# Gates moved between the two halves of a head's q, k, v projection, in a gated attention layer on one NeuronCore

## The chip, the core and the metric

The kernel runs on one core of one Trainium2 chip. The time is the device time of one execution in microseconds (us); three runs are shown for the kernel before, and their median is the number to predict against. One further execution was recorded by the hardware profiler, and all rows below come from that one. Engines are called PE (TensorE matmul), DVE (VectorE), ACT (ScalarE), POOL (GpSimd) and SP (SyncE, which here only issues DMAs).

## The reference, cut to what matters

With DEPTH = 1 only the first layer runs: 1024 tokens, 1024 features, 16 heads with a value width of 128 and two query/key pairs of width 64 each.

```python
def diff_attention_layer(x, norm_g, w_in, q_norm_g, k_norm_g, ..., head_norm_g, w_out, layer_idx):
    h = rms_norm(x, norm_g)
    q, k, v, z = jnp.split(h @ w_in, 4, axis=-1)
    q = rms_norm(q.reshape(b, s, DA_HEADS, 2, DA_HEAD), q_norm_g) * (DA_HEAD ** -0.5)
    k = rms_norm(k.reshape(b, s, DA_HEADS, 2, DA_HEAD), k_norm_g)
    ...
        scores = einsum('bqhmd,bkhmd->bhmqk', qb, kb)          # per block of 128 queries, causal
        probs = softmax(scores + alibi_bias)
        weights = probs[:, :, 0] - lam * probs[:, :, 1]
        outs.append(einsum('bhqk,bkhe->bqhe', weights, vb))
    ...
    o = rms_norm(o, head_norm_g) * (1.0 - lam_0)
    o = o.reshape(b, s, BRANCH) * jax.nn.silu(z)
    return x + o @ w_out
```

## The kernel before, in words

**Products.** Each f32 operand is split into two f16 parts, hi and lo, and a product is three matmuls (hi·hi, hi·lo, lo·hi) that add up in PSUM. The normalised input stands transposed in SBUF as `h0` and `h1`, for the first and the last 512 tokens; index `c` is 0 or 1 for these halves.

**Prologue.** Eight tiles of x are normalised (`htok`, L259), transposed on PE (`tp`, L275) and split by ACT (L277) and DVE (L278) into `h`. The first head's projection starts before all eight are there: the scheduler puts its matmuls between the transposes.

**Heads.** They run in the order 1, 3, .., 15, 0, 2, .., 14. While head i is projected, head i−1 is attended: `merge` (L656) draws pieces of both by the costs that they yield and the rates in `RATE`; then the tile scheduler fixes the order of instructions on each engine. `project` (L354) does, for each half `c`: four token tiles, 24 matmuls each of 128x384 into a PSUM tile `pg` (L370 to L372); ACT copies q, k out (L422) and v (L423); DVE makes the low part of v, `vl` (L424). Then `norm(c, rw)`: ACT squares (L381), DVE sums (L383), POOL multiplies by the gain (L385), a small chain for 1/sqrt (L90 to L103), DVE multiplies (L388), ACT and DVE split (L391, L392), SP transposes (L393) and copies. After both halves come the gates: `gate(st, wt, 3, c)` (L443), 24 matmuls of 128x512 into `pz` (L447 to L449) and a chain of six steps that gives z·sigmoid(z) in `sz`: ACT exp (L452), DVE min (L453), ACT ln (L454), DVE (L455), ACT exp (L456), DVE (L457). `pz` is read by the last step, so its PSUM slot is free only then. `pg` and `pz` share one ring of three PSUM slots (`PSG` = 3, tag "pg").

The heads 10, 12, 14 (`LATE`) have no gates in `project`; `late_gates` (L510) computes them at the end, while head 14 is attended, and beside them splits the first half of `w_out` (`wo_half`, `split_wo`; DVE subtraction L467 into `wol`).

**Preparation of w_in.** The raw weights of the next head come by SP DMAs (L136) into the single buffer `raww`. `split_w` (L141) is a generator that `prepare` advances one step at a time: four squares on ACT (L160), a small chain with one PE matmul into spare columns of a `pg` tile (L169), then hi on ACT (L199), and lo on DVE (L205, blocks q and k) or on POOL (L202 and L203, blocks v and z). Before, it is advanced after each token tile and at every second step of the gates; the first head, which also has its own z block to prepare, advances it at each half tile.

**Attention.** `attend` (L540) goes through eight blocks of 128 queries: scores on PE (L570) into `pss` (four PSUM slots), DVE takes them out with the bias and a running minimum (L559), ACT exp (L576), DVE combines the two softmaxes (L581, L582, L584), ACT and DVE split (L66, L587), SP transposes. Values on PE (L601 to L603), then the head norm (L607 to L631, POOL L614) and `finalize` (L529), in which POOL multiplies with the gate (L537) and SP writes to DRAM.

**End.** The second half of `w_out` and the products with the gathered heads (`pf`, L498 to L500).

## Time and profile before

| | us |
|---|---|
| runs before | 1181.22, 1174.27, 1176.29 |
| median | 1176.29 |
| profiled execution, own time | 1173.53 |
| its span (first to last instruction) | 1171.8 |
| PE busy in the span | 1109.9 (95%) |
| DVE busy | 883.0 (75%) |
| ACT busy | 774.2 (66%) |
| POOL busy | 272.2 (23%) |

The profiled execution takes 1.7 us beyond its span and lies 2.8 us below the median. The mean clock that TensorE was granted over the span is 0.983 of full speed. A row of the timeline reads: start, duration, engine, line, operation, output<-inputs, and in brackets the idle time of that engine just before, with what ended it. Rows of waits read: engine, what it was about to write and its line, `<-` what it waited for, total us, times, longest.

### The profile page before, as it was taken

What the parts mean: (1) busy time and instruction counts of PE and PEld (TensorE: products, weight loads), DVE (VectorE), ACT (ScalarE), POOL (GpSimd) and SP (SyncE); (2) the same over time, 40 slices, a digit from 0 to 9 for tenths busy, and PEclk for the clock granted to TensorE, in tenths of its full rate; (3) what the DMA queues carried; (4) which work ended last, traced back from release to release, by engine and by line L of the source; (5) the groups of instructions that cost most, each with busy time, mean ns of one, the idle gap of its engine ahead of it and who ended that gap; (6) DMA issues with size and microseconds to landing.
All of it is one profiled execution on the core that took longest, in us unless ns stands there. A gap on an engine that the chain in (4) does not pass through costs nothing.

```text
span 1171.8 us, 18439 instructions
## 1 busy us (share of the span) xinstructions
PE 1109.9 (95%) x6154; PEld 668.5 (57%) x6154; DVE 883.0 (75%) x2180; ACT 774.2 (66%) x1713; POOL 272.2 (23%) x208
## 2 busy tenths in 40 slices
PE   4999999999999999999999999999899997999998
PEld 3555554545555555555545455555455534788887
DVE  6867869787978797879787878788888898563121
ACT  4757778787878797869686978787778776230000
POOL 2220314141314131314131313312121302031000
PEclk7999999999999999999999999999999988999999
DMA  7453736464646464646463645464564457685342
GB/s 222 109 119 52 164 67 140 89 140 85 139 90 137 88 143 89 146 80 133 93 144 76 140 93 126 93 129 100 105 137 87 109 125 182 143 292 179 112 130 70
DMA packets 327887, 143.50 MB, mean 122 GB/s; under 512 B 225136, under 2 KB 307312, under 8 KB 327792
## 3 DMA queue, kind: packets, MB, share of 16 engines
q1 hardware_dynamic: 323040, 133.93, 50.9%
q10 hardware_dynamic: 4752, 8.39, 2.7%
q8 instruction: 48, 0.79, 0.3%
q14 instruction: 47, 0.39, 0.1%
HBM read 63.11 MB, written 16.25 MB: 68 GB/s over the span
## 4 chain that ended last, share of the span: by engine, by line
PE 51%; DVE 20%; ACT 10%; issue 8%; DMA 6%; POOL 2%; SPq 2%; DVEq 0%; ACTq 0%; POOLq 0%
PE pg L370 8%; PE pg L371 8%; PE pg L372 8%; DVE p L559 6%; PE pf L498 5%; PE pf L499 5%; PE pf L500 5%; PE pss L570 3%; DMA raww<-in_l_w_in_dram 3%; DVE p L584 2%; ACT p L576 2%; ACT wsp L160 2%; ACT wsp L199 2%; DMA wt<-p 2%; PE po L601 2%
## 5 line engine op out<-in xcount | busy, mean ns | idle before, releaser
L370 PE MATMUL pg<-wsp,h 128*128 128x384 f16 x1024 | 336.3, 328 | 21.0 <-DVE sz L457 11.9
L372 PE MATMUL pg<-wsp,h 128*128 128x384 f16 x1024 | 336.4, 329 | 1.1 <-DVE h L278 1.1
L371 PE MATMUL pg<-wsp,h 128*128 128x384 f16 x1024 | 336.3, 328 | 1.2 <-POOL wsp L203 1.2
L576 ACT ACTIVATE p<-p,mn 128x128 f32<-128x128 f32 (+7 forms) x256 | 196.4, 768 | 61.0 <-DVE mn L559 59.8
L559 DVE CUSTOM_DVE_ANT_0 p<-pss,toep,nsl 128x512 f32<-128x512 f32 (+3 forms) x256 | 161.2, 642 | 36.8 <-DMA wt<-p 24.6
L570 PE MATMUL pss<-qk 128*128 128x512 f16 (+3 forms) x768 | 164.6, 327 | 11.6 <-DVE mn L559 11.5
L371 PEld LDWEIGHTS <-h 128*128 128x128 f16 x1024 | 100.7, 98 | 86.7 <-issue 26.5
L372 PEld LDWEIGHTS <-h 128*128 128x128 f16 x1024 | 100.6, 98 | 68.2 <-issue 3.7
L66 ACT ACTIVATE p<-p,rc 128x128 f16<-128x128 f32 (+7 forms) x128 | 98.6, 771 | 61.8 <-DVE p L584 60.7
L370 PEld LDWEIGHTS <-h 128*128 128x128 f16 x1024 | 100.7, 98 | 66.6 <-issue 4.1
L584 DVE SCALAR_TENSOR_TENSOR p<-p,rc,p 128x128 f32<-128x128 f32 (+7 forms) x128 | 116.9, 914 | 1.5
L587 DVE SCALAR_TENSOR_TENSOR p<-p,rc,p 128x128 f16<-128x128 f32 (+7 forms) x128 | 104.7, 820 | 14.8 <-ACT p L66 14.6
L570 PEld LDWEIGHTS <-qk 128*128 128x128 f16 x768 | 71.0, 98 | 72.2 <-issue 18.6
L447 PE MATMUL pz<-h,wsp 128*128 128x512 f16 x256 | 98.3, 384 | 1.3 <-DVE sz L457 1.3
L448 PE MATMUL pz<-h,wsp 128*128 128x512 f16 x256 | 98.3, 384 | 0.0
L614 POOL TENSOR_TENSOR sql<-sqo,sqh 128x512 fp32r<-128x512 f32 x30 | 41.7, 1390 | 243.3 <-ACT sqh L612 243.3
L449 PE MATMUL pz<-h,wsp 128*128 128x512 f16 x256 | 98.1, 383 | 0.0
L537 POOL TENSOR_TENSOR sz<-sqo,sz 128x512 f32<-128x512 f32 x26 | 37.7, 1448 | 184.4 <-DVE sqo L631 150.0
L202 POOL TENSOR_SCALAR raww<-raww,scw 128x1024 f32<-128x1024 f32 (+1 forms) x31 | 42.3, 1371 | 159.1 <-ACT wsp L199 127.9
L559 DVE CUSTOM_DVE_ANT_0 p<-pss,toep,mn 128x128 f32<-128x128 f32 (+3 forms) x128 | 75.6, 601 | 0.0
L160 ACT ACTIVATE wsp<-raww 128x1024 f16<-128x1024 f32 x61 | 63.6, 1044 | 14.7 <-DMA raww<-in_l_w_in_dram 9.4
L503 DVE TENSOR_TENSOR xr<-pf,xr 128x512 f32<-128x512 f32 (+1 forms) x33 | 22.1, 671 | 63.4 <-PE pf L500 62.5
(160 smaller groups left out, 2082.9 us busy)
## 6 DMA issues: line engine op xcount, KB each, us to landing
raww<-in_l_w_in_dram SPq DMA_DIRECT2D x96, 256.0 KB, 3.8
rawo<-in_l_w_out_dram SPq DMA_DIRECT2D x32, 256.0 KB, 4.5
qk<-qk SPq DMA_DIRECT2D x64, 128.0 KB, 2.4
raww<-in_l_w_in_dram SPq DMA_DIRECT2D x40, 192.0 KB, 3.7
g_dram<-sz SPq DMA_DIRECT2D x30, 256.0 KB, 2.3
rawg<-g_dram ACTq DMA_DIRECT2D x24, 256.0 KB, 3.5
xt<-in_x_dram SPq DMA_DIRECT2D x8, 512.0 KB, 5.3
xr<-in_x_dram SPq DMA_DIRECT2D x16, 256.0 KB, 3.5
```

The source lines that it names most:

```text
L66: A.activation(out, in_, AF.Copy, scale=scale)
L370: T.matmul(pg, a_h, w_h, start=k == 0, stop=False)
L371: T.matmul(pg, a_h, w_l, start=False, stop=False)
L372: T.matmul(pg, a_l, w_h, start=False, stop=k == KT - 1)
L447: T.matmul(pz, wt["hi"][:, k, n], hh[c][:, k], start=k == 0, stop=False)
L448: T.matmul(pz, wt["hi"][:, k, n], hl[c][:, k], start=False, stop=False)
L449: T.matmul(pz, wt["lo"][:, k, n], hh[c][:, k], start=False, stop=k == KT - 1)
L559: V.tensor_tensor_reduce(out=pm[m][:, o:o + w], in0=pss[:, :w], in1=toep[:, u:u + w], scale=nslope, scalar=3e38 if prev[m] is None else pr ...
L570: T.matmul(pss[m][:, :w].rearrange("p (t q) -> p t q", q=P), qk[:, c, 0, i % 4, m], qk[:, b, v, :w // P, m], start=v == 1, stop=v == 2)
L576: A.activation(pm[m][:, :n], pm[m][:, :n], AF.Exp, scale=-1.0, bias=prev[m], accum_out=sx[:, 1 - m:2 - m])
L584: V.scalar_tensor_tensor(out=p0, in0=p1, scalar=rc[:, 0:1], in1=p0, op0=ALU.mult, op1=ALU.add)
L587: V.scalar_tensor_tensor(out=pl[:, n:], in0=p0, scalar=rc[:, 1:2], in1=pl[:, :n], op0=ALU.mult, op1=ALU.subtract)
```

## The change

`project` is written in another order. `qkv(c)` is the former loop body. Heads outside `LATE` now run `qkv(0)`, both gates, `qkv(1)`; before, `qkv(0)`, `qkv(1)`, both gates. `prepare(None)` at half a tile is now called for every head, but only with c = 0: of the next head's preparation 8 calls stand in `qkv(0)`, 8 in the gates and 4 in `qkv(1)`. The ring of `sz` has four buffers instead of three. The temporary `sqo` of the head norm no longer has a tile of its own; it takes the first 512 columns of the ring "sqk" (2 buffers), which `norm` and the out-projection use. Lines from 441 on have a number lower by one in the changed kernel.

```diff
-            for c in range(2):
+            def qkv(c):
                 rw = tmp.tile([P, 2, 4, P], F32, name="rw", tag="rw", bufs=2)
                 for t in range(4):
...
                             prepare(lambda: pb[:, 384:])
-                        elif hd == heads[0]:
+                        elif c == 0:
                             prepare(None)
                         yield 2.1
                 norm(c, rw)
-            if hd in LATE:
-                while prep:
-                    prepare(None)
-                return
-            for c in range(2):
-                for k in gate(st, wt, 3, c):
-                    if k % 2:
-                        prepare(None)
-                    yield 0.69
+            yield from qkv(0)
+            if hd not in LATE:
+                for c in range(2):
+                    for k in gate(st, wt, 3, c):
+                        if k % 2:
+                            prepare(None)
+                        yield 0.69
+            yield from qkv(1)
             while prep:
                 prepare(None)
...
-            e = vp.tile([P, 512], F32, name="sz", tag="sz", bufs=3)
+            e = vp.tile([P, 512], F32, name="sz", tag="sz", bufs=4)
...
-                sq = tmp.tile([P, 512], F32, name="sqo", tag="sqo")
+                sq = tmp.tile([P, 1024], F32, name="sqo", tag="sqk", bufs=2)[:, :512]
```

What the scheduler makes of it, at three places. The numbers behind names tell buffers apart.

PE in the prologue, before: `tp_514` and `tp_521` are the transposes of the last x tile, `pg_766` and `pg_796` are tiles of the first head's half c = 1. Between `tp_507` and `tp_514` stand 26 matmuls here.

```order
L372 MATMUL pg_766<-wsp_206,h1_84 128x384
L169 MATMUL pg_722<-br_735,ones_63 128x4
L370 LDWEIGHTS h1_84
L370 MATMUL pg_796<-wsp_206,h1_84 128x384
L371 LDWEIGHTS h1_84
L371 MATMUL pg_796<-wsp_206,h1_84 128x384
L275 MATMUL tp_514<-ident_65,htok_498 128x128 x4
L275 MATMUL tp_521<-ident_65,htok_498 128x128 x4
```

The same place after; `pz_721` and `pz_755` are the gates of the first head.

```order
L448 MATMUL pz_721<-h0_83,wsp_206 128x512
L275 MATMUL tp_500<-ident_65,htok_405 128x128 x4
L275 MATMUL tp_507<-ident_65,htok_405 128x128 x4
L275 MATMUL tp_514<-ident_65,htok_498 128x128 x4
L275 MATMUL tp_521<-ident_65,htok_498 128x128 x4
L446 LDWEIGHTS wsp_206
L446 MATMUL pz_755<-h1_84,wsp_206 128x512
L370 LDWEIGHTS h1_84
L370 MATMUL pg_788<-wsp_206,h1_84 128x384
```

Now 24 gate matmuls stand ahead of the four transposes in a row (22 of them behind the transposes of the tile before), the second gate's first matmul right behind them, and the first head's c = 1 tiles after that.

DVE in a head of the middle, before: the end of gate 0's chain (`sz_5507`), up to the step that frees its PSUM slot.

```order
L388 TENSOR_TENSOR rw_5137<-rw_5137,r_k_5419 128x1024
L455 SCALAR_TENSOR_TENSOR sz_5507<-pz_5427,inv_4307,sz_5507 128x512
L581 RECIPROCAL rc_5535<-sums3_461 128x2
L582 TENSOR_TENSOR rc_5535<-rc_5535,sums3_461 128x2
L559 ISA p0_5558,mn_5567<-pss_5561,toep_407,nsl_432 128x128
L559 ISA mn_5567 128x1
L559 ISA p1_5559,mn_5569<-pss_5562,toep_407,nsl_432 128x128
L559 ISA mn_5569 128x1
L584 SCALAR_TENSOR_TENSOR p0_5481<-p1_5482,rc_5535,p0_5481 128x1024
L631 SCALAR_TENSOR_TENSOR sqo_5389<-os_5387,gh_416,sqo_5389 128x512
L392 TENSOR_TENSOR sqk_5407<-rw_5137,sqk_5407 128x16x64
L457 SCALAR_TENSOR_TENSOR sz_5507<-pz_5427,inv_4307,sz_5507 128x512
```

The same place after (`sz_5903`):

```order
L388 TENSOR_TENSOR rw_5585<-rw_5585,r_k_5812 128x1024
L454 SCALAR_TENSOR_TENSOR sz_5903<-pz_5820,inv_4935,sz_5903 128x512
L583 SCALAR_TENSOR_TENSOR p0_5885<-p1_5886,rc_5939,p0_5885 128x640
L558 ISA p1_5947,mn_5956<-pss_5949,toep_407,nsl_432 128x512
L558 ISA mn_5956 128x1
L452 TENSOR_SCALAR sz_5980<-sz_5980 128x512
L392 TENSOR_TENSOR sqk_5800<-rw_5585,sqk_5800 128x16x64
L558 ISA p1_5947,mn_5972<-pss_5965,toep_407,mn_5956,nsl_432 128x256
L558 ISA mn_5972 128x1
L456 SCALAR_TENSOR_TENSOR sz_5903<-pz_5820,inv_4935,sz_5903 128x512
```

The norm that stands in the chain is now that of half 0, the softmax steps beside it are those of smaller query blocks, and the second gate's first step (`sz_5980`) stands ahead of the first gate's last.

DVE near the end, while head 14 is attended, before: the subtractions L467 for the first half of `w_out` stand between the last scores' evacuations.

```order
L559 ISA p1_11144,mn_11153<-pss_11146,toep_407,nsl_432 128x512
L559 ISA mn_11153 128x1
L467 TENSOR_TENSOR wol1_11252<-rawo_11277,woh1_11251 128x512
L629 SCALAR_TENSOR_TENSOR t1_10912<-os_10858,gh_416,sqo_10860 128x512
L584 SCALAR_TENSOR_TENSOR p0_10969<-p1_10970,rc_11018,p0_10969 128x640
L559 ISA p0_11143,mn_11173<-pss_11167,toep_407,mn_11151,nsl_432 128x384
L559 ISA mn_11173 128x1
L467 TENSOR_TENSOR wol1_11252<-rawo_11281,woh1_11251 128x512
L559 ISA p1_11144,mn_11175<-pss_11168,toep_407,mn_11153,nsl_432 128x384
```

The same place after:

```order
L558 ISA p0_11143,mn_11173<-pss_11167,toep_407,mn_11151,nsl_432 128x384
L558 ISA mn_11173 128x1
L466 TENSOR_TENSOR wol1_11252<-rawo_11257,woh1_11251 128x512
L558 ISA p1_11144,mn_11175<-pss_11168,toep_407,mn_11153,nsl_432 128x384
L558 ISA mn_11175 128x1
L558 ISA p0_11189,mn_11197<-pss_11191,toep_407,nsl_432 128x512
L558 ISA mn_11197 128x1
L558 ISA p1_11190,mn_11199<-pss_11192,toep_407,nsl_432 128x512
```

Of the six subtractions into `wol1` five now stand behind the evacuation `mn_11175`, where before all six stood ahead of it; the head norm's L628 (L629 before) and a gate's last step have moved behind it too.

## Rows read from the trace of the kernel before

**Rows 1.** Page, busy time, share of the span and instructions.

```profile
PE 1109.9 (95%) x6154; PEld 668.5 (57%) x6154; DVE 883.0 (75%) x2180; ACT 774.2 (66%) x1713; POOL 272.2 (23%) x208
```

**Rows 2.** Stretches: us from the start, length, busy per engine, clock, DMA share, GB/s.

```profile
117.00:800.00 683.00, 664.84 (x3858) 371.08 (x3856) 566.74 (x1422) 534.90 (x1190) 181.81 (x119) 1.00 0.55 113
937.00:996.00 59.00, 48.33 (x212) 24.31 (x211) 53.31 (x122) 40.38 (x85) 10.05 (x9) 0.88 0.65 152
```

**Rows 3.** Waits of PE from 117 to 800 us: total, times, longest.

```profile
PE pg L370 <- DVE sz L457: 11.5, 7, 2.3
PE pg L370 <- DVE vl L424: 5.1, 5, 1.6
```

**Rows 4.** Waits of PE from 937 to 996 us.

```profile
PE pss L570 <- DVE mn L559: 6.0, 6, 2.5
PE pmn L621 <- POOL sql L614: 2.2, 1, 2.2
PE pz L447 <- DVE sz L457: 1.3, 1, 1.3
PE pf L498 <- POOL gt L70: 1.1, 1, 1.1
```

**Rows 5.** Timeline of PE in the prologue: start, duration.

```profile
45.42 1.04 PE L275 MATMUL tp<-ident,htok 128*128 128x128 f32 x8
...
52.38 0.34 PE L372 MATMUL pg<-wsp,h 128*128 128x384 f16 x1 [1.14 <-DVE h L278]
...
59.31 1.94 PE L275 MATMUL tp<-ident,htok 128*128 128x128 f32 x8 [2.13 <-DVE htok L259]
```

**Rows 6.** Timeline of DVE, the last x tile's normalisation.

```profile
57.89 1.28 DVE L259 SCALAR_TENSOR_TENSOR htok<-xt,r_x,gb 128x1024 f32<-128x1024 f32 x1
```

**Rows 7.** Timeline of PE in the second head.

```profile
92.03 0.27 PE L570 MATMUL pss<-qk 128*128 128x128 f16 x2 [1.42 <-DVE mn L559]
```

**Rows 8.** Timeline of PE in a middle head: first gate's last matmuls, the slot wait.

```profile
243.50 0.38 PE L448 MATMUL pz<-h,wsp 128*128 128x512 f16 x1
243.72 0.38 PE L449 MATMUL pz<-h,wsp 128*128 128x512 f16 x1
...
258.12 0.32 PE L370 MATMUL pg<-wsp,h 128*128 128x384 f16 x1 [2.27 <-DVE sz L457]
```

**Rows 9.** Timeline of POOL and DVE in the same head.

```profile
237.69 4.22 POOL L203 TENSOR_TENSOR wsp<-raww,wsp 128x1024 f16<-128x1024 f32 x2
...
237.81 0.17 DVE L581 RECIPROCAL rc<-sums 128x2 f32<-128x2 f32 x1 [0.81 <-ACT p L576]
...
238.55 1.29 DVE L582 TENSOR_TENSOR rc<-rc,sums 128x2 f32<-128x2 f32 x1
...
239.97 0.73 DVE L559 CUSTOM_DVE_ANT_0 p<-pss,toep,nsl 128x512 f32<-128x512 f32 x1
...
240.63 2.10 DVE L584 SCALAR_TENSOR_TENSOR p<-p,rc,p 128x768 f32<-128x768 f32 x1
...
246.73 0.15 DVE L582 TENSOR_TENSOR rc<-rc,sums 128x2 f32<-128x2 f32 x1
...
257.32 0.74 DVE L457 SCALAR_TENSOR_TENSOR sz<-pz,inv,sz 128x512 f32<-128x512 f32 x1
```

**Rows 10.** Groups of DVE from 117 to 800 us: busy us, mean ns.

```profile
L205 DVE SCALAR_TENSOR_TENSOR wsp<-raww,scw,wsp 128x1024 f16<-128x1024 f32 x24 | 29.9, 1278 | 1.3 <-ACT wsp L199 1.3
```

**Rows 11.** Groups of DVE by shape from 915 to 993 us.

```profile
L467 DVE TENSOR_TENSOR wol<-rawo,woh 128x512 fp32r<-128x512 f32 x12 | 10.7, 900 | 1.1 <-ACT woh L466 1.1
L457 DVE SCALAR_TENSOR_TENSOR sz<-pz,inv,sz 128x512 f32<-128x512 f32 x6 | 4.4, 738 | 0.4 <-ACT sz L456 0.4
...
L559 DVE CUSTOM_DVE_ANT_0 p<-pss,toep,mn 128x256 f32<-128x256 f32 x4 | 2.1, 530 | 0.0
...
L584 DVE SCALAR_TENSOR_TENSOR p<-p,rc,p 128x640 f32<-128x640 f32 x2 | 1.8, 875 | 0.0
...
L584 DVE SCALAR_TENSOR_TENSOR p<-p,rc,p 128x1024 f32<-128x1024 f32 x1 | 1.3, 1271 | 0.0
```

## The prediction, as it was put on record

> **What bounds the kernel now.** The page first: PE is busy 1109.9 of 1171.8 us [rows 1], so all that the change can win is among some 62 us in which PE waits, and it removes no matmul. The table of stretches then says where these lie. From 117 to 800 us, twelve heads, PE is busy 664.84 of 683.00 us at full clock, DVE 566.74 [rows 2]: 18 us of waiting. From 937 to 996 us PE has 48.33 of 59.00 while DVE has 53.31 [rows 2]: there DVE is the bound. The waits of PE name what comes last. In the middle stretch it is nearly one thing: the first matmul of a projection tile waits for a PSUM slot, seven times until L457 has read the gate (11.5 us), five times until L424 has read a tile (5.1 us), 16.6 us in all [rows 3]. Near the end the scores wait for their evacuation, 6.0 of 10.6 us [rows 4]. The timeline of one middle head shows how a slot wait arises. Gate 0's last matmul starts at 243.72; PE does 12.1 us of other work and stands 2.27 us before 258.12 [rows 8]. DVE is without a gap from 237.81 to the end of L457 at 258.06 [rows 9]: the gate's chain is short, but in DVE's queue it stands between 20 us of softmax and norm. So a head's wait is DVE's work from the last evacuation that it did on time up to L457, less PE's work up to the third tile after the gate.
>
> **Part 1, the prologue: a loss.** Before, the wait for the last x tile is filled with the first head's c = 1 tiles; its `htok` is ready at 57.89 + 1.28 = 59.17 [rows 6], and PE lost 1.14 and 2.13 us there [rows 5], 3.3 us. After, PE goes the same way up to the transposes at 45.42 [rows 5], then has 22 gate matmuls at 0.22 us [rows 8], 4.8 us, and four transposes of one x tile, 1.04 us [rows 5]: it is at `tp_514` at 46.5 + 4.8 + 1.0 = 52.3. ACT and DVE have the same queue as before up to the chain of the last tile, but for the gate's first exp and min, which stand ahead of it now; I give them 0.4 us. PE waits from 52.3 to 59.6, 7.3 us, then some 1.0 us for the split of that tile, which `pz_755` needs and `pg_796` did not (the like wait took 1.14). That is 8.3 + 0.3 less 3.3: **+5.3 us**. The last transposes take 1.94 us instead of 1.04 after a wait of 2.13 us [rows 5]: the granted clock has fallen to its lower level, 1.2 GHz. A wait of 7 us can cost another dip, of which 0 to 1.7 us are lost; I take 0.9. In the second head PE lost 1.42 us to an evacuation, behind squares that waited for raw weights [rows 7]; after, the scores of the first head stand closer together beside the gates, and by counts DVE is 2.4 us late there once: +0.6. Part 1 is **+6.8**, between +3 and +11.
>
> **Part 2, twelve middle heads: a gain.** The gate's place moves, so it has other neighbours. After, the ring goes gate 0, gate 1, tile, tile: the second tile of `qkv(1)` waits for gate 0's L457. I counted the order for two heads in a row, since they alternate. Tight head: DVE's rows from the evacuation that it does on time to L457 gain two L205 (2 × 1.28 [rows 10]), two evacuations of 256 (2 × 0.53), an L453 (0.4), softmax steps L584 and L587 of 640, 512 and 384 columns, and lose those of 1024, 896 and 768. A step has 0.875 us at 640 and 1.271 at 1024 [rows 11], by a straight line 0.61 at 384 and 1.01 at 768, and L587 is priced alike. Added 2.56 + 1.06 + 0.4 + 0.875 + 2 × (0.74 + 0.61) = 7.6; removed 1.27 + 2 × 1.14 + 2 × 1.01 = 5.6; net +2.0. PE's work over the same distance gains 12 value matmuls, 1.6 us, and scores of 1.0 us: +2.6. The tight head is eased by 0.6 us, between 0.3 and 0.9. The other kind has a shorter list on both sides and comes out 0.4 to 1.3 us easier; I take 0.6, since its wait before was only 5.1 / 5 = 1.0 us and a later tile is left with little room. Sum: 7 × 0.6 + 5 × 0.6 = **−7.2 us** of the 16.6. The bounds are −16.6, all of it, and +16, below.
>
> One thing in DVE's list is no constant. In rows 9 L582 takes 1.29 us beside POOL's L203 and 0.15 later; L584 of 768 columns takes 2.10 against 1.01 by the line: 1.14 + 1.09 = 2.2 us a head. An evacuation in the same stretch, which reads PSUM and one tile of SBUF, has 0.73 [rows 9] and isn't slowed. POOL's preparation stands 8 us of PE's work ahead of gate 0's end instead of 10.5; in both orders DVE has no gap from there to L457, so I cost the move at nothing. The cover is that the 2.2 us are paid in the chain already; if they weren't, they are a rival.
>
> The Trainium skill, page "SBUF — State Buffer", section "Who interferes with whom", says that a DVE instruction with two SBUF inputs contends with a GpSimd instruction that reads SBUF, and that the one that comes second is blocked entirely. The trace agrees: 1.29 against 0.15 us for such an instruction, 0.73 us for one with an input in PSUM [rows 9]. By this rule a move of preparation into the gates speaks against the change, since L584, L587, L388 and L392 stand in the gate's chain: where a lock falls newly into it, twelve heads at 2.2 us would give 26 us, and the sum would end near 1195 instead of 1168.5.
>
> **Part 3, near the end: a gain.** From the first of head 14's long evacuations to the last, DVE has five L467 less (5 × 0.90), one L457 and one L629 (0.74 each, the same shape) less, one L587 of 640 (0.875) and one small step more [rows 11]: 4.5 + 1.48 − 1.0 = 5.0, less 0.07 for each of five overlaps, 4.6 us, against the same PE work of 56 us. DVE is late there throughout, so the waits of 10.6 us [rows 4] shrink by **−4.6**. The five subtractions come later, where PE has the products with `w_out` before it and DVE has room. Between −8 and +2: the waits could move to those products.
>
> **Part 4, buffers.** A fourth `sz` releases a wait that no row of PE, and none of the gate's steps, shows; `sqo` in the ring of `sqk` makes L609 wait for the transposes L393 of two norms earlier and L381 for a `finalize`. Both have half a head of room. Queued behind L609 on ACT is L612 and what follows of the softmax; if the cover fails, each case would cost about one L381 and its chain, 1 to 2 us a head. SP's raw loads are issued earlier in the head, and its transposes L589 stand behind them; they wait for the softmax longer than the loads wait for POOL. Nothing for each.
>
> The Trainium skill, page "Perfetto Trace Analysis", section "Optimization Strategy", says that a gap which repeats on the engine that should be saturated can mean too few SBUF or PSUM buffers. The trace has such a gap, and it is for a slot of the three in PSUM [rows 3]. The fourth buffer of the change is in SBUF: by the page it would cure nothing here, and the sum without it is the same.
>
> **Sum.** +6.8 − 7.2 − 4.6 = −5.0 on 1173.53 us: 1168.5. The median of the runs shown lies 2.8 above the profiled execution, so **1171.3 us**.
>
> **Rivals.** *Slot waits gone:* gate 0's chain gets enough room that both waits of rows 3 vanish; for it speaks that DVE has 17% free in the stretch, against it that L457 stays behind 20 us of DVE work. 1173.5 + 6.8 − 16.6 − 4.6 + 2.8 = 1161.9. *A lock in the chain (slower):* POOL's L202 and L203 fall newly into gate 0's chain and each head pays up to 2.2 us. It decides from the point where L203 still runs when gate 0's last matmul ends. For it: the preparation now runs beside the gates. Against: the lock lies in the same gapless stretch before. In the seven tight heads 15.7 us, without Part 2's gain: 1173.5 + 6.8 − 4.6 + 15.7 + 2.8 = 1194.2; in all twelve near 1205. *The waits only move:* the tile after next is late instead, or the end gives its gain back. 1173.5 + 6.8 − (0 to 4.6) + 2.8 = 1178.5 to 1183. *No effect of the move:* the scheduler could have undone it; the order shows that it did not.
>
> **Chances.** Forecast 0.43 (its own range 1166 to 1176), slot waits gone 0.20, waits only move 0.22, lock 0.15. A measurement of this kernel can tell about 0.5%, 5.9 us, from no change, so faster means under 1170.4. Faster: 0.20 and a little under half of the forecast, 0.39. Slower, above 1182.2: the lock and part of the moved waits, 0.24. Same: 0.37. The range of 8 in 10 goes from 1161, the case without slot waits, to 1188, halfway into the lock.
>
> **What would show it.** Part 1: a gap of 7 to 8 us before the last x tile's transposes, near 52 to 60 us. Part 2: PE's waits for L456 and L424 from 117 to 800 us at 9 to 10 us instead of 16.6; at 0 the first rival, above 25 the lock, then with L583 or L586 steps of 2 us behind gate 0's last matmul. Part 3: waits for evacuations near the end of 6 us in all. The prediction is wrong if the slot waits stay and only the prologue's loss remains, or if a wait appears for `sqk` or for SP.

## The result, and the profile after

The changed kernel takes 1183.64 us in the median (1181.26 to 1186.63) against 1174.71 us (1172.08 to 1181.22) of the kernel before, on the same chip: 1.0074 times the time before, with a 95% interval of 1.0056 to 1.0092. Forecast were 1171.3 us and a gain; it is a loss of 9 us, inside the range of 1161 to 1188 but on the other side of no change.

First the stretches of the profiled execution (start and end, length, then busy time and count of PE, weight loads, DVE, ACT, POOL, then clock, DMA share, GB/s), to be read against [rows 2]; its span is 1179.5 us.

```profile
47.00:62.00 15.00, 6.79 (x39) 4.02 (x37) 11.30 (x45) 11.32 (x25) 2.49 (x2) 0.85 0.32 84
...
117.00:800.00 683.00, 654.88 (x3762) 364.32 (x3761) 567.83 (x1387) 518.62 (x1157) 183.65 (x117) 0.99 0.54 111
...
937.00:996.00 59.00, 53.35 (x258) 26.99 (x258) 53.43 (x133) 43.27 (x93) 7.92 (x8) 0.97 0.62 136
```

From 117 to 800 us PE is busy 10 us less than before; from 937 to 996 us it is busy 5 us more. The waits of PE in the changed kernel, first from 117 to 800 us, to be read against [rows 3]:

```profile
PE po L600 <- DMA wt<-p: 16.4, 9, 3.1
PE pss L569 <- DVE mn L558: 7.6, 10, 1.9
PE pss L569 <- DMA qk<-qk: 2.0, 2, 1.7
PE po L600 <- ACT sqk L391: 1.8, 1, 1.8
PE pg L370 <- DVE sz L456: 0.4, 2, 0.2
```

The slot waits of 16.6 us are gone but for 0.4. In their place the value product (`po`, L600) waits 16.4 us for the transposed softmax weights (18.2 with the 1.8 us that the view puts down to L391 and that ended as such a transpose landed), and the scores wait 7.6 us for their evacuation. Near the end, 937 to 1003 us, against [rows 4]:

```profile
PE pz L446 <- DVE sz L456: 3.9, 1, 3.9
PE pss L569 <- DVE mn L558: 0.9, 2, 0.5
PE po L600 <- ACT sqo L622: 0.9, 1, 0.9
PE po L600 <- ACT sums L577: 0.8, 1, 0.8
PE pf L497 <- POOL gt L70: 0.8, 1, 0.8
```

That is 7.3 instead of 10.6 us. Since the order differs, stretches of the clock don't hold the same work. So the two traces were laid side by side by PE's work: for each matmul in its place in the order, the columns of all matmuls before it, and its start in the trace.

| share of PE's columns | start before, us | after minus before, us | change in the part, us | forecast for it |
|---|---|---|---|---|
| 3.4% (last x tile done) | 69.40 | +4.9 | +4.9 | +5.3 and 0.9 of clock |
| 7.6% (second head) | 118.07 | +2.8 | −2.1 | +0.6 |
| 13.3% | 179.07 | +18.2 | **+15.4** | in Part 2 |
| 70% (end of the heads with gates) | 812.84 | +20.7 | +2.5 | −7.2 |
| 83% | 961.89 | +16.0 | −4.7 | |
| 85% (scores done) | 994.04 | +7.4 | −8.6 | −4.6 |
| 100% | 1168.38 | +7.4 | 0 | |

### The profile page after: what moved, and what is told of

Same layout as the page of the kernel before. It is cut to its first block, busy times and chain, and to the rows that moved or that the text cites. A ratio compares the mean times of both kernels' runs of the same rounds, so it can differ in the third digit from the quotient of the medians.

```text
span 1179.5 us, 18382 instructions
## 1 busy us (share of the span) xinstructions
PE 1112.2 (94%) x6154; PEld 671.0 (57%) x6154; DVE 894.5 (76%) x2180; ACT 769.8 (65%) x1713; POOL 278.1 (24%) x208
## 4 chain that ended last, share of the span: by engine, by line
PE 69%; DVE 14%; DMA 8%; issue 5%; ACT 2%; SPq 1%; POOL 1%; DVEq 0%; ACTq 0%; POOLq 0%
PE pg L370 11%; PE pg L372 11%; PE pg L371 11%; PE pss L569 7%; PE pf L497 5%; PE pf L498 5%; PE pf L499 5%; DMA wt<-p 4%; DVE p L558 3%; PE pz L446 3%; PE pz L448 3%; PE pz L447 3%; PE po L600 2%; PE po L601 2%; PE po L602 2%
## 5 line engine op out<-in xcount | busy, mean ns | idle before, releaser
L569 PE MATMUL pss<-qk 128*128 128x512 f16 (+3 forms) x768 | 168.0, 330 | 11.2 <-DVE mn L558 8.8
L586 DVE SCALAR_TENSOR_TENSOR p<-p,rc,p 128x128 f16<-128x128 f32 (+7 forms) x128 | 108.3, 848 | 10.3 <-ACT p L66 10.3
L583 DVE SCALAR_TENSOR_TENSOR p<-p,rc,p 128x128 f32<-128x128 f32 (+7 forms) x128 | 109.8, 866 | 1.1
L613 POOL TENSOR_TENSOR sql<-sqo,sqh 128x512 fp32r<-128x512 f32 x30 | 40.3, 1344 | 233.7 <-ACT sqh L611 233.7
L202 POOL TENSOR_SCALAR raww<-raww,scw 128x1024 f32<-128x1024 f32 (+1 forms) x31 | 48.9, 1586 | 181.8 <-ACT wsp L199 142.1
L600 PE MATMUL po<-wt,vh 128*128 128x512 f16 x192 | 64.0, 334 | 21.9 <-DMA wt<-p 18.4
L536 POOL TENSOR_TENSOR sz<-sqo,sz 128x512 f32<-128x512 f32 x26 | 44.3, 1703 | 167.8 <-DVE sqo L630 115.5
L199 ACT ACTIVATE wsp<-raww,scw 128x1024 f16<-128x1024 f32 (+1 forms) x67 | 69.0, 1099 | 3.6 <-DVE scw L180 3.5
```

Source lines behind the costliest of these rows:

```text
L569: T.matmul(pss[m][:, :w].rearrange("p (t q) -> p t q", q=P), qk[:, c, 0, i % 4, m], qk[:, b, v, :w // P, m], start=v == 1, stop=v == 2)
L583: V.scalar_tensor_tensor(out=p0, in0=p1, scalar=rc[:, 0:1], in1=p0, op0=ALU.mult, op1=ALU.add)
L586: V.scalar_tensor_tensor(out=pl[:, n:], in0=p0, scalar=rc[:, 1:2], in1=pl[:, :n], op0=ALU.mult, op1=ALU.subtract)
```

## The parts of the change, one at a time

**Buffers alone.** The kernel before with the two buffer edits.

```diff
-            e = vp.tile([P, 512], F32, name="sz", tag="sz", bufs=3)
+            e = vp.tile([P, 512], F32, name="sz", tag="sz", bufs=4)
-                sq = tmp.tile([P, 512], F32, name="sqo", tag="sqo")
+                sq = tmp.tile([P, 1024], F32, name="sqo", tag="sqk", bufs=2)[:, :512]
```

> The kernel before with the two buffer edits alone (fourth sz, sqo in the ring of sqk). Theory A, that the order of qkv and gates carries everything, expects no difference: 1.000, and the waits of PE from 937 to 996 us at 10 to 11 us as before. Theory B, that the gain near the end (the changed kernel is 13 us quicker than before between the matmuls at 69% and 84% of PE's work) comes from the buffers, expects 0.990 to 0.993, with those waits at 5 to 7 us.

Measured 1.0022 (1.0007 to 1.0037). The buffers bring nothing in the old order, and at most 0.4% of loss: the gain near the end isn't theirs, though the waits from 937 to 1003 us, 8.1 us, lie between the two theories.

**Order alone.** qkv(0), gates, qkv(1), preparation and buffers as before.

```diff
-                        elif c == 0:
+                        elif hd == heads[0]:
                             prepare(None)
```

> The order alone: qkv(0), gates, qkv(1), with the preparation called as before and the old buffers. Theory A expects the changed kernel's time, 1.006 to 1.009, with no slot wait for gates left from 130 to 800 us, value matmuls waiting 15 to 20 us for the transposed weights, and some 10 us of waits from 120 to 200 us. Theory C, that the moved preparation and its lock on DVE carry the loss, expects 0.992 to 0.998 and the waits of value matmuls under 5 us.

Measured 1.0602 (1.0571 to 1.0634): neither theory. The same with the new buffers:

> The changed kernel with the preparation called as before. Theory A expects 1.006 to 1.009 (the same as the changed kernel). Theory C expects 0.99 to 0.997: what remains is the order's and the buffers' gain.

Measured 1.0548 (1.0523 to 1.0573): neither again. With this order the buffers bring about 0.5% (1239.8 against 1245.5 us in the median); whether they do in the changed kernel wasn't tried. PE's waits in the run with the order alone, 117 to 800 us:

```profile
PE pg L370 <- DVE vl L424: 32.0, 13, 3.6
PE pss L569 <- DVE mn L558: 18.9, 11, 3.1
PE pg L370 <- DVE sz L456: 10.1, 9, 4.1
PE pg L370 <- ACT wsp L199: 2.4, 7, 0.3
```

The code says why: the matmul L169 needs a `pg` tile, and only the call after a whole token tile brings one. With four calls in `qkv(0)` the four squares take them all; the eight calls in the gates find no tile and do nothing, and the rest is done in a lump at the head's end, where the tiles then wait. So the half-tile calls are no second idea but what makes the new order bearable: they are worth 5%.

**Preparation alone**, order as before.

```diff
-                        elif hd == heads[0]:
+                        elif c == 0:
                             prepare(None)
```

> The preparation alone: called at the first half's half tiles for every head, order of qkv and gates and buffers as before. Theory A expects 0.998 to 1.002 with the slot waits near 16 us. Theory C expects 1.005 to 1.010, with L205 at 1.4 to 1.5 us in the mean instead of 1.28 and a busier DVE (890 us or more).

Measured 1.0017 (1.0000 to 1.0033), no difference in sum, though it is one of two parts. Laid side by side with before it loses 6.9 us between 7.6% and 9.5% of PE's work, where one wait of 3.2 us for q and k and a dip of the clock stand, and gains 7.7 us from 70% to 76%, where heads without gates are projected. The second part alone:

```diff
-                        elif hd == heads[0]:
+                        elif hd == heads[0] or hd in LATE and c == 0:
                             prepare(None)
```

> The kernel before, with the moved preparation in the three LATE heads alone (their first halves), nothing else. In the run with the preparation moved in all heads the stretch of these heads came out 8 us shorter, and the second and third head 7 to 9 us longer. If both are local effects, this run expects 0.992 to 0.995 of the kernel before. If the gain there is only lost time given back (PE catching up on waits of earlier heads), it expects 0.999 to 1.001.

Measured 0.9957 (0.9940 to 0.9973), a gain, just short of the first expectation. The trace shows 7.2 us won from 70% to 76%, as expected, and 3.5 us given back later. In the changed kernel the same stretch wins 4.4 us; this edit can account for that.

**First head in the old order**, the rest as changed.

```diff
-                        elif c == 0:
+                        elif c == 0 or hd == heads[0]:
                             prepare(None)
...
             yield from qkv(0)
+            old = hd in heads[:1]
+            if old:
+                yield from qkv(1)
             if hd not in LATE:
...
-            yield from qkv(1)
+            if not old:
+                yield from qkv(1)
```

> The changed kernel with the first head alone in the old order (both projection halves, then its gates). The prologue's term was put at +5.3 us and measured +5.0 at the point where PE has done 4% of its work, of which 2.2 to 2.8 are left after the second head. If that term is local, this run is 2 to 6 us quicker than the changed kernel: 1.002 to 1.006 of the one before, and the 8 us gap ahead of the last x tile is gone. If the loss of some 15 us in the second and third head hangs on the first head's order, it is 10 us or more quicker: under 0.999.

Measured 1.0039 (1.0021 to 1.0057): 4 us quicker than the changed kernel. The prologue's term is local and about as big as forecast; the 15 us of the second and third head are not in it (17.8 us between 7.6% and 13.3% in this run).

## What makes the middle slow

The changed kernel's trace of one middle head, POOL, DVE, SP and PE (timelines, rows left out; the last `L586` is the last softmax step of the fourth query block, which the value product needs last):

```profile
288.05 1.27 POOL L613 TENSOR_TENSOR sql<-sqo,sqh 128x512 fp32r<-128x512 f32 x1 [13.93 <-ACT sqh L611]
291.61 3.17 POOL L202 TENSOR_SCALAR raww<-raww,scw 128x1024 f32<-128x1024 f32 x2 [2.29 <-ACT wsp L199]
294.76 2.13 POOL L203 TENSOR_TENSOR wsp<-raww,wsp 128x1024 f16<-128x1024 f32 x1
296.85 1.27 POOL L385 TENSOR_TENSOR rw<-rw,gain 128x512 f32<-128x512 f32 x1
298.07 2.14 POOL L203 TENSOR_TENSOR wsp<-raww,wsp 128x1024 f16<-128x1024 f32 x1
302.95 1.69 POOL L536 TENSOR_TENSOR sz<-sqo,sz 128x512 f32<-128x512 f32 x1 [2.74 <-DVE v_k L100]
...
288.27 1.08 DVE L190 TENSOR_SCALAR ep<-ep,sg 128x16 f32<-128x16 f32 x1
...
291.87 1.93 DVE L205 SCALAR_TENSOR_TENSOR wsp<-raww,scw,wsp 128x1024 f16<-128x1024 f32 x1
...
296.92 1.23 DVE L96 SCALAR_TENSOR_TENSOR v_k<-ssk,ep 128x16 f32<-128x16 f32 x1
...
298.46 1.84 DVE L581 TENSOR_TENSOR rc<-rc,sums 128x2 f32<-128x2 f32 x2
...
303.40 1.27 DVE L101 SCALAR_TENSOR_TENSOR v_k<-v_k,y_k 128x16 f32<-128x16 f32 x1
...
305.42 0.74 DVE L586 SCALAR_TENSOR_TENSOR p<-p,rc,p 128x512 f16<-128x512 f32 x1
...
306.19 1.23 SPq L588 DMA_TRANSPOSE wt<-p  x1
...
309.38 0.38 PE L600 MATMUL po<-wt,vh 128*128 128x512 f16 x1 [2.11 <-DMA wt<-p]
```

Five entries of DVE, six instructions, take 7.35 us; alone they have 0.2, 1.28, 0.17, 2 × 0.15 and 0.17, about 2.1 us. Each lies beside a POOL instruction, but only L205 and L581 beside the weight steps L202 and L203, and these lose 2.2 us; L190, L96 and L101 lose 3.0 us beside L613, L385 and L536, which the head norm, the projection's norm and the gate product have in any order. So the lock is 5 us in this head, not 2.2, and it stands ahead of the softmax step that the value product needs. SP issues the transpose at 306.19, when L586 is done, and PE gets the weights 2.1 us late.

Over the same work of the heads with gates (7.6% to 70%), DVE instructions that ran over 0.1 us longer than the quick ones of their line and shape lost 40 us in the kernel before and 52 in the changed one, every one of them beside a POOL instruction; beside L202 and L203 it is 26 and 25. What the lock adds is 12 us, none of it beside the moved weight steps.

That is not yet why the value product waits. The traces show where it stands in PE's order, and when the softmax of the fourth block is done (third to tenth head):

| kernel | softmax done, us behind the fourth block's scores | value product, us of PE's work (columns at 2.4 GHz) behind them |
|---|---|---|
| before | 10.1 to 14.5 | 26.1 |
| changed, heads in turn | 13.5, 15.3 | 18.0, 15.8 |
| changed, low parts on DVE (below) | 11.8, 16.1 to 16.8, 13.2 to 13.5 | 17.1, 21.4, 18.2 |

The softmax comes 1.7 us later in the mean (14.4 against 12.7); the product stands 8 to 10 us nearer. Before, the transposes had 12 to 16 us; now they have 4.5 or 0.5, and those that ended the waits took 3.1 to 5.5 us from issue to landing. Of the waits, 12.5 us fall where SP issued the transpose within 0.12 us of the softmax's last step, as in the head above: DVE is late there. The other 5.7 us are four waits whose transposes were ready and stood 1.0 to 2.5 us while SP issued raw loads. Neither the order alone (34 us of work) nor the preparation alone (31) puts the product so near, and neither waits more than 2.2 us for these weights; it is the two together, by the scheduler's times.

**All low parts on DVE**, none on POOL, in the changed kernel and, as the control, in the kernel before:

```diff
-LO_POOL = (2, 3)
+LO_POOL = ()
```

> The changed kernel with the low parts of all four weight blocks made by DVE (L205), none by POOL. DVE gets two more instructions of 1.2 us a head, POOL loses some 6.6 us a head. Theory L, that POOL's weight steps beside the gates hold DVE up (in one middle head five DVE instructions took 5.2 us longer than alone) and so make the softmax late, expects the value matmuls' waits at under 6 us instead of 16 and 0.990 to 0.996 of the changed kernel. Without that lock as a cause, 2.4 us more DVE work a head makes it slower: 1.005 to 1.02 of the changed kernel.

> The same edit on the kernel before, as the control: there DVE lost 2.2 us a head beside POOL's steps, about what the edit adds, so 0.998 to 1.004 by theory L; 1.005 to 1.02 if the added DVE work counts and the lock does not.

Measured 0.9793 (0.9769 to 0.9817) of the kernel before, 1149.6 us, and 0.9843 (0.9821 to 0.9865), 1154.8 us. Both gain more than theory L forecast, though DVE has two more instructions of 1.3 us a head; the control's range went by the lock's 2.2 us a head, so the lock's own time doesn't account for it. And the sign of the change turns: with low parts on DVE the new order is 0.5% quicker than the old, with low parts on POOL 0.7% slower. But the scheduler's order is another too: the table above has the softmax half a microsecond earlier in the mean (13.9) and the product 2 us further behind (19.0 against 16.9), and some 5 us left for the transposes in every head. The changed kernel without POOL's steps, 117 to 800 us, stretch and waits:

```profile
117.00:800.00 683.00, 681.91 (x3996) 384.63 (x3995) 590.93 (x1503) 543.95 (x1227) 97.55 (x77) 1.00 0.57 118
```

```profile
PE pss L569 <- DMA qk<-sqk: 0.6, 1, 0.6
PE po L600 <- DMA wt<-p: 0.2, 1, 0.2
```

PE is busy 681.91 of 683 us. The mean of the short DVE instruction on the softmax factors shows the lock in each kernel, 130 to 800 us (busy us, mean ns), first before, then changed, then changed without POOL's steps:

```profile
L582 DVE TENSOR_TENSOR rc<-rc,sums 128x2 f32<-128x2 f32 x92 | 27.4, 298 | 1.3
```

```profile
L581 DVE TENSOR_TENSOR rc<-rc,sums 128x2 f32<-128x2 f32 x90 | 32.2, 362 | 2.4 <-ACT sums L577 1.0
```

```profile
L581 DVE TENSOR_TENSOR rc<-rc,sums 128x2 f32<-128x2 f32 x96 | 16.5, 172 | 1.7
```

But the loss that comes back with POOL isn't the lock alone. Three runs bear on it, each adding POOL work to the kernel with low parts on DVE, behind L205 in the code: reads that hold the raw buffer, writes that hold it, and reads that hold nothing of it.

```diff
+                        if s_ >= 2 and not first:
+                            for _ in range(2):
+                                G.tensor_scalar(src, src, c_, 1.0, ALU.mult, ALU.mult)
```

> The kernel with all low parts on DVE (1149.6 us), plus four POOL instructions a head that scale raw weights in place, which nobody uses: they stand in POOL's queue where L202 and L203 stood and hold the raw buffer, some 5.4 us a head. Theory L (POOL reading SBUF holds DVE up) expects the loss to come back in large part: 0.990 to 1.005 of the kernel before, with L581 and other short DVE instructions at 1 to 2 us beside them. Theory Q (late low parts of the weights were the cause, not the lock) expects 0.977 to 0.983, since the weights are DVE's now. If POOL's queue or the later release of the raw buffer is the cause, it comes back here and in the run with writes alike.

```diff
+                        if s_ >= 2 and not first:
+                            for _ in range(2):
+                                G.memset(src, 0.0)
```

> The same with four POOL instructions a head that only write (zeros into the used raw buffer), in the same places of the queue. Theory L expects 0.977 to 0.984, the time without them, and no long DVE instructions beside them. A cause in POOL's queue or in the raw buffer's release expects the same loss as in the run with reads, scaled by their length.

```diff
+                        if s_ >= 2 and not first:
+                            for k_ in range(KT):
+                                sx_ = wsm.tile([P, P], F16, name="scr", tag="scr", bufs=1)
+                                G.tensor_tensor(sx_, l_[:, k_], h_[:, k_], ALU.subtract)
```

> All low parts on DVE (1149.6 us), plus 32 short POOL subtractions a head that read finished weights and write a scrap tile: nobody waits for them and they don't hold the raw buffer. Theory L (POOL's reading of SBUF holds DVE up, and that alone is the cost) expects 0.990 to 1.005 of the kernel before, near the 1.018 or 1.001 of the runs that held the raw buffer too. Theory S (POOL releases the single raw buffer late, the raw loads wait at the head of SP's queue, and the transposes of the softmax behind them come late) expects 0.979 to 0.984, the time without them.

Measured 1.0183 (1.0161 to 1.0205), 1.0010 (0.9993 to 1.0027) and 0.9881 (0.9859 to 0.9903). POOL in the last one reads 106 us from 117 to 800 us, no less than the changed kernel's L202 and L203:

```profile
L210 POOL TENSOR_TENSOR scr<-wsp 128x128 f16<-128x128 f16 x192 | 106.0, 552 | 76.6 <-DVE wsp L205 32.7 <-DVE un L365 31.3
```

Reading that nobody waits for costs 0.9%, some 10 us of the 33, which lies between the forecasts of both theories. Writing that holds the raw buffer costs 2.2%, and reading that holds it 3.9%, more than theory L allows. So more goes with holding the buffer than with reading. The two runs hold it longer than the changed kernel does, since POOL waits for L205 there: SP stands 99 and 78 us for POOL at raw loads (130 to 800 us), and 65 in the changed kernel. Nor does the lock's sum go with the time: 45 us in the run with reads that hold nothing, 37 and 28 where POOL holds the buffer, 52 in the changed kernel, 15 without POOL's steps.

SP's queue doesn't carry it alone either. SP's waits ahead of raw loads, 130 to 800 us, before and in the changed kernel:

```profile
SPq L136 <- POOL wsp L203: 65.2, 12, 6.3
SPq L136 <- DVE wsp L205: 12.5, 10, 1.6
```

```profile
SPq L136 <- POOL wsp L203: 64.8, 11, 6.4
SPq L136 <- DVE wsp L205: 57.2, 10, 11.7
```

What has grown is the wait for DVE, not for POOL. Between the softmax step and the issue of its transpose there lie in sum 23.5 us before, 40.5 in the changed kernel, 22.4 without POOL's steps, but also 23.7 in the slow run with reads and 38.4 in the quicker one of the old order with all low parts on DVE.

And the scheduler makes another order each time: with reads that hold the buffer the value product stands 15.4 to 22.9 us behind. The four kernels in which POOL holds the buffer and the changed order runs from the first head on (the changed one, reads, writes, and the one with one block on POOL, below) all lose 11 to 15 us between 7.6% and 13.3%; with nothing held it is 0.2 and 1.0. The changed kernel there, two stretches:

```profile
120.80:148.60 27.80, 23.42 (x129) 13.12 (x127) 22.27 (x54) 18.83 (x45) 5.45 (x3) 0.88 0.83 170
148.60:197.30 48.70, 42.49 (x235) 22.71 (x234) 35.26 (x79) 31.37 (x67) 14.34 (x9) 0.96 0.38 85
```

and its waits of PE, in the timeline:

```profile
127.45 0.22 PE L569 MATMUL pss<-qk 128*128 128x128 f16 x1 [1.17 <-DVE mn L558]
129.18 0.22 PE L569 MATMUL pss<-qk 128*128 128x128 f16 x1 [1.51 <-DVE mn L558]
131.10 0.82 PE L569 MATMUL pss<-qk 128*128 128x128 f16 x4 [1.71 <-DMA qk<-qk]
```

Waits of 1.2 to 1.7 us follow each other here, one of 3.1 us for transposed weights later, and the granted clock is 0.88 of full speed in one stretch and 0.96 in the next: of the 15.4 us, 10.6 are waits and 4.8 slower matmuls. The kernel before has no wait and the full clock over the same work. How much of the part beyond 10 us is the late release itself and how much the other order, these runs don't separate.

The Trainium skill, page "SBUF — State Buffer", section "Who interferes with whom", has a write-only GpSimd instruction leave alone a DVE instruction with two SBUF inputs, but has DVE's two-port modes contend with any GpSimd instruction. The run with writes agrees with the first: the two-input step on the softmax factors (L581 in the changed kernel) has 151 ns in the mean beside such a write and 154 with nothing of POOL beside it. It fits the second, if the one-input minimum of the gate (L452) runs in such a mode, which no row tells: 1147 ns in the mean beside a write against 418.

**One block on POOL instead of two:**

```diff
-LO_POOL = (2, 3)
+LO_POOL = (3,)
```

> The changed kernel with POOL making the low part of one block a head (z) instead of two. If the cost goes with the time of POOL's weight steps, half of the 33 us between the changed kernel and the one with all low parts on DVE comes back: 0.990 to 0.996 of the kernel before. If it is a threshold (slack that is used up), the result is near one of the ends, 0.979 to 0.984 or 1.004 to 1.008.

Measured 1.0005 (0.9992 to 1.0018), in neither forecast: the first block taken away gives 8 us, the second 25. It doesn't go with POOL's time. The 14 us between 7.6% and 13.3% are still there, and go only with the second block; that POOL frees the raw buffer at all may be the reason, and isn't shown apart from the order.

**Raw loads by ACT's queue**, to free SP (the edit on the changed kernel, the call cut short):

```diff
-                ins = Q.dma_start(raw[:, k, bs], ...)
+                q_ = Q if hd == heads[0] else A
+                ins = q_.dma_start(raw[:, k, bs], ...)
```

> The changed kernel, low parts on POOL as it has them, with the raw loads of all heads but the first issued by ACT's queue instead of SP's: a load that waits for POOL no longer stands ahead of the transposes. Theory S expects 0.985 to 0.998 of the kernel before, with the value matmuls' waits at under 6 us; theory L expects 1.003 to 1.010, as the changed kernel; if the loads hold up ACT instead, it is slower than that.

Measured 1.0390 (1.0366 to 1.0413), the third outcome, and 1.0463 (1.0433 to 1.0493) for the same edit on the kernel before, where 0.993 to 1.004 was expected by one theory or the other. ACT spends 54 and 55 us from 130 to 800 us on issuing these loads. The value product still waits 23.4 us, though SP now issues the transposes that end these waits within 0.24 us of the softmax: in this run it isn't SP's queue that makes them late.

**Value product one block later:**

```diff
-VALUES_AT = 5
-NORM_AT = 6
+VALUES_AT = 6
+NORM_AT = 7
```

> The changed kernel, with the first value product one block of queries later (after step 6 instead of 5) and its head norm one later too. Theory V, that the value matmuls come too early for softmax weights that DVE now finishes late, expects the 16 us of waits for transposed weights from 130 to 800 us to fall under 4 us and 0.990 to 0.996 of the changed kernel (0.997 to 1.003 of the one before). Its rival, that DVE is simply full there and any matmul that depends on it waits, expects the wait under another name (scores, projection slots), 12 us or more in all, and a time within 0.3% of the changed kernel.

Measured 1.0198 (1.0174 to 1.0221). The value product's wait halves, from 16.4 to 8.1 us, and the scores' waits for evacuations go from 7.6 to 21.1. The rival's wait under another name came, its time did not: the run is 1.2% slower than the changed kernel. And theory V wasn't tried: in the order that the scheduler made, the product stands 15.4 or 18.3 us of work behind the fourth block's scores, about as near as before the edit.

**A step more ahead of DVE's wait.** In the changed kernel DVE stands 28.5 us at L172 for the small matmul L169 (0.3 before).

```diff
             T.matmul(pb[:, :n + n % 2], ones, br[:, :n + n % 2], start=True, stop=True)
+            if not first:
+                yield
```

> The changed kernel with one more step of the preparation between the small matmul L169 and DVE's first instruction on its result (L172), so that DVE reaches that instruction half a tile later. In the changed kernel DVE stands 28.5 us at L172 from 62 to 800 us, ten times, where before it stood 0.3. Theory W, that this standing makes the softmax late, expects the wait under 8 us, the value matmuls' waits at half or less, and 0.995 to 1.003 of the kernel before. If DVE would have been idle there anyway and the time beside POOL counts, 1.005 to 1.010 as the changed kernel.

Measured 1.0078 (1.0060 to 1.0095), but the wait is still 27.5 us: in the trace every engine has the order of instructions that it had. The theory wasn't tried by it and stays open.

**First heads in the old order.** All low parts on DVE with the first head in the old order:

> All low parts on DVE, the changed order, and the first head in the old order. If the prologue's loss (with the low parts on DVE it is +9.4 us at 2.5% of PE's work against +4.2 in the old order, and +4.9 against -4.2 at 8%) is local, this gives 0.970 to 0.975 of the kernel before, the quickest of all; if PE catches up on it later anyway, 0.977 to 0.981.

Measured 0.9831 (0.9809 to 0.9853), in neither range. The prologue's gain is there and lost again where the new order begins, by a slot wait of 3.6 us and a wait for q and k of 1.9. With the first two heads in the old order (`heads[:2]` in the edit above, and no half-tile calls in the second):

> All low parts on DVE, the first two heads in the old order with the preparation as before, the others in the new. With the first head alone in the old order the prologue's gain of 9 us was lost again at 8 to 10% of PE's work, where the first head in the new order begins. If that loss belongs to the passage from old to new, it comes here too, one head later: 0.980 to 0.985. If it belongs to the second head in the new order, it is gone: 0.970 to 0.976.

Measured 0.9760 (0.9743 to 0.9777), 1147.1 us. The loss one head later is 3.3 us instead of 9, so it belonged mostly to the second head in the new order; the second head's preparation is the old one too. This version beats both kernels, the changed one by 3%. Its interval overlaps that of the changed order throughout with low parts on DVE (0.9769 to 0.9817), so that it is the quicker of these two isn't clear.

## Why the prediction was wrong

**Part 1's gap held in size.** The gap ahead of the last x tile is there (timeline of PE, against [rows 5]):

```profile
61.38 1.94 PE L275 MATMUL tp<-ident,htok 128*128 128x128 f32 x8 [8.21 <-DVE htok L259]
```

8.2 us against 7.3 forecast, +4.9 us in all against +5.3 and 0.9 for the clock; the dip of the clock came in both kernels. In the second head PE won 2.1 us instead of losing 0.6, so Part 1 came to +2.8 in sum, against +6.8 and a lower bound of +3.

**Part 2 failed, and with it the sign.** Its direct claim was too timid: the slot waits fell by 16.2 us, not by 7.2, as the first rival had it. The step that failed is "PE's work over the same distance gains 12 value matmuls": they were booked as work that PE can do ahead of the slot, without asking whether their weights are there. The same shift brings the value product from 26.1 to 15.8 or 18.0 us behind the fourth block's scores, nearer than the softmax and its transposes allow, and it waits 16.4 us; the scores wait 7.6 instead of 0.8. "The waits only move" was a rival with 0.22, priced at 1178.5 to 1183; the measurement lies just above it. From 13.3% to 70% of the work the change is worth +2.5 us, nothing like −7.2.

**The lock was costed at nothing, which held for the weight steps alone.** Beside them it is 26 and 25 us over twelve heads, alike in both orders, as Part 2 said; but DVE loses 12 us more beside POOL's other steps, and Part 2 priced only the gate's chain. The same stretch of DVE holds the softmax of the value product, which had 12 us or more to spare before and has at most 4.5 now. The rival "a lock in the chain" put its price on the slot; what the lock costs fell on another wait. Shown: with POOL's weight steps gone, and the order that the scheduler then makes, the waits are gone and the sign of the change turns. Shown too: a run with reading alone loses 10 of 33 us. Not shown: what splits the rest between the held buffer, the lock and the order.

**The early heads were not in the sum at all.** I counted the order for two heads in the steady middle and multiplied by twelve. The second and third head lost 15.4 us, more than the whole change. That is a term left out, not one mis-sized. Where POOL holds nothing and the first head is in the new order, at most 1 us is lost there; why holding the buffer costs it stays open.

**Part 3 was right, and the clock added to it:** −8.6 us from 83% to 85% against −4.6. The waits in that part went from 8.0 to 2.1 us, 5.9 less; the other 2.7 us are quicker matmuls, at a granted clock of 1.00 instead of 0.89, which the sum did not have. Part of what surrounds it has another source: the half-tile calls in the three heads without gates, 7 us there and 5 in the end when tried alone. Part 4 put the moved preparation at nothing on SP's queue; SP stands 122 us ahead of raw loads instead of 78, and the transposes are issued 17 us later in sum. "They wait for the softmax longer than the loads wait for POOL" failed for the four transposes that stood behind raw loads and held PE up, 5.7 us. The buffers were rightly put near nothing in the old order; in the new one that is not shown.

## What to carry to other kernels

When a change removes the wait that comes last, price the next consumer of the same busy engine before booking the gain. Matmuls that come into a stretch are work for PE only if their inputs are ready: count how far they stand behind what makes these inputs, before and after. Here a wait for a PSUM slot became one for softmax weights, since the product had come 8 to 10 us nearer to them. Count the orders of the first heads apart from the steady ones; they have other neighbours. And ask of a helper engine not only whether it keeps up, but what it holds meanwhile: moving two weight blocks a head from an engine that was 23% busy to one that was 75% busy made the two kernels 1.6% and 2.8% quicker.

## What the runs showed of the hardware

Short DVE instructions on 2 to 16 columns take 0.15 to 0.2 us, and 1.1 to 1.3 us in the rows shown (up to 1.9 for L581) where they meet a POOL `tensor_tensor` that reads SBUF. POOL loses as well: its 128x128 subtraction has 0.43 us in the median and 1.29 or more in the longest twentieth. POOL's zeros over 128x1024 f32 take 0.96 us; eight one-input minima of DVE on 128x512 beside them have 1.15 us in the mean, 13 with nothing of POOL beside them 0.42, and L205 keeps its 1.28 there. A stretch of 28 us with three waits of PE, 4.4 us in all, had a granted clock of 0.88, where the same work without waits had 1.00.
